# One 64-column decode step for the eight delta-net heads of a hybrid decoder, with the state update placed beside the branch projections

## The chip, the cores and the metric

The kernel is one launch on 1 core of one Trainium2 chip. The metric is device time in microseconds (us), the median of three runs. Nothing of the computation is split over cores, so one span and one chain of waits tell the whole story.

## The reference, cut to what matters

One layer of a hybrid decoder is computed for 256 prompt tokens and 8 sample sequences of one token each. The 264 token columns go through the same weights together: a half-step SwiGLU, a mixer (gated delta-net and sliding-window attention, each projected and merged under a gate), a cross attention over 256 memory tokens, and a second SwiGLU. The change is in the sample tokens' part of the delta-net, which for one token per sequence is a single step per head on a 128 x 128 state:

```python
S_t = a_t (I - b_t k_t k_t^T) S_{t-1} + b_t k_t v_t^T
o_t = S_t^T q_t
o_g = rms_norm(o_t, gdn_norm) * silu(z)
```

There are 8 heads and 8 sample sequences, so 64 such steps, and 64 new states (4 MB in all) must be written out. The query and key are l2-normalised first. In the kernel's form one needs the products of the old state with k and q, then u = b (v - a S^T k), the output from S^T q and the dot product of k and q, and the new state a S + k u^T.

## The kernel before, in words

All activations lie transposed: 128 channels on the partitions, 264 token columns. A weight matrix is streamed once from memory in 512 KB pieces. `wsplit` (L157) loads a piece on SyncE's queue into `raw` (4 buffers), ScalarE rounds it to `wh` (L162, 3 buffers) and VectorE computes the remainder `wl` (L163, 4 buffers). `gemm` (L177) then issues three matmuls for each 128 x 128 block, wh with xh, wh with xl and wl with xh (L194 to L196). These lines are called the weight matmuls below, and everything else on TensorE the small matmuls. Weight matmuls fill TensorE for nearly the whole launch.

The mixer (L285) is where other work must fit in between. It lists its steps in a string, "c0 c1 s c2 w0 c3 w1 x w2 w3":

- `c0` to `c3`: for a pair of heads, `conv_pair` (L452) projects k, q, v and the gate z, applies the short convolution, and leaves them in `kp`, `qp`, `vp`, `zp`. `gdn_pair` (L479) does the chunked delta rule of the 256 prompt tokens, a long chain of small matmuls and VectorE steps that ends with a reciprocal square root (thirteen short VectorE operations), a scaling (L652), four transposes (L655) and the write of `og` (L656). `gdn_sample` (L658) then does the decode step of the pair's 16 columns.
- `s`: the projections for sliding-window attention. `w0` to `w3`: `swa_prompt` (L806) for one group of key heads, in three blocks of scores (L821), softmax, transposes (L842) and values (L848). `x`: `swa_sample` (L852), which goes through the caches in four pieces for the keys (L877) and four for the values (L907), in the three `kc` buffers; the row of the newest value is written into each value piece by a second transfer (L903).

After the steps come sixteen projections of the gate logits (`gate`, L914), of which twelve belong to the stage of the small work and the last four follow once buffers are handed over; then the two branch projections (`branches`, L936) and the output projection `w_out`.

`gdn_sample` as it stands, for each pair of heads: four states of 256 KB are loaded on SyncE's queue (L672) into the pair's own work buffers `d`, `T`, `U`, `bv`; one matmul with a matrix of ones sums squares (L689); four matmuls of 32 columns by 512, one for each loaded state, write four different groups of 32 partitions of one accumulator (L698); a mask and two additions pick the wanted parts; a transpose (L704) brings them back; u is formed, transposed (L719) and written to a small tensor `ud` in device memory (L723); the outputs are normalised (L726 sums the squares) and go to `og`. Then each `ud` row is loaded back, spread over 128 partitions (L737), into `ke` and `u`, ScalarE scales state and spread row (L740, L741, eight operations for each 256 KB), VectorE adds them (L742) and GpSimd's queue stores the new state (L743).

The order of the work is not the order of the code. A list scheduler in the build sets each engine's order from the data dependences, the buffers (a tile of a pool is taken in program order and waits until the tile before it in the same buffer is done with) and its own timing. Each engine then runs its list strictly in order: what waits at the head holds all that stands behind it.

Of the kernel before, what the change touches and what calls it, by code (L numbers as in the profile page):

```python
# [6 lines left out]
F32 = mybir.dt.float32  # L7
# [8 lines left out]
P = 128  # L16
# [53 lines left out]
def bc(ap, n):  # L70
    return ap[:, :, None].to_broadcast([ap.shape[0], ap.shape[1], n])
# [6 lines left out]
class Build:  # L78
# [206 lines left out]
    def mixer(self, norm, nxt):  # L285
# [7 lines left out]
        self.gp = self.mid.enter_context(self.phase("gp", 2))  # L293
        gates = [(n, g) for n in range(2) for g in range(8)]
        if True:
            with self.phase("mc") as mc, self.phase("gd", 2, PSUM) as gd, self.phase("sw", 2, PSUM) as sw:
                self.mc, self.gd, self.sw = mc, gd, sw
                self.c = mc.tile([P, C_N - P], F32, name="c")
                nc.gpsimd.dma_start(out=self.c, in_=i["cst"][:, P:])
                self.scalars_load()  # L300
                self.gemm_ba(win, xs)
                self.conv_state_load()
                for step in "c0 c1 s c2 w0 c3 w1 x w2 w3".split():
                    k = int(step[1:] or 0)
# [18 lines left out]
            with self.phase("bp", 3) as bp:  # L323
# [36 lines left out]
    def gemm_ba(self, win, xs):  # L360
# [65 lines left out]
        nc.vector.tensor_copy(out=self.sbg.rearrange("p a h b -> p (a h b)"), in_=pb[:, 0:128])  # L426

# [230 lines left out]
    def gdn_sample(self, p):  # L658
        nc, mc, o, i = self.nc, self.mc, self.o, self.i
        idn = self.K(C_ID)  # L660
        hsl = slice(2 * p, 2 * p + 2)
        sc = slice(NP, TOK)
        n = 2 * NS
        TT = nc.vector.tensor_tensor
        STT = nc.vector.scalar_tensor_tensor
        st = lambda name, m=n: mc.tile([P, m], F32, name=name)
        v2 = lambda t: t.rearrange("p (h b) -> p h b", h=2)
        Ss = []
        for h in range(2):
            for hb in range(2):  # L670
                S = self.gt(("d", "T", "U", "bv")[h * 2 + hb])
                nc.sync.dma_start(out=S, in_=i["state_gdn"][2 * p + h, :, hb * 4:hb * 4 + 4])  # L672
                Ss.append(S)
        kqz = self.gt("w", 2)[:, 0].rearrange("p (m c) -> p m c", m=4)
        nc.vector.memset(kqz[:, :, 8:32], 0.0)
        kq = kqz[:, :, 0:8].rearrange("p (h r) (b two) -> p h r b two", h=2, two=2)
        cp = lambda src: src.rearrange("p h (r b) -> p h r b", r=2)
        f2 = lambda t: t.rearrange("p (h r b) -> p h r b", h=2, r=2)
        pr = mc.tile([P, 3, n], F32, name="pr")
        vs = st("vs")  # L680
        nc.vector.tensor_copy(out=kq[:, :, :, :, 0], in_=cp(self.kp[:, :, sc]))
        nc.vector.tensor_copy(out=kq[:, :, :, :, 1], in_=cp(self.qp[:, :, sc]))
        nc.vector.tensor_scalar(out=v2(vs), in0=self.vp[:, :, sc], scalar1=0.5, scalar2=None, op0=ALU.mult)
        kk, qq = self.kp[:, :, sc], self.qp[:, :, sc]
        TT(out=v2(pr[:, 0]), in0=kk, in1=kk, op=ALU.mult)
        TT(out=v2(pr[:, 1]), in0=qq, in1=qq, op=ALU.mult)
        TT(out=v2(pr[:, 2]), in0=kk, in1=qq, op=ALU.mult)
# [11 lines left out]
        xm, own = self.gt("E1"), self.gt("sq")[:, 0]
        TT(out=xm, in0=pX.rearrange("p (b e) -> p b e", b=4), in1=bc(self.K(C_DG, 4), P), op=ALU.mult)  # L700
        TT(out=xm[:, 0:2], in0=xm[:, 0:2], in1=xm[:, 2:4], op=ALU.add)
        TT(out=own, in0=xm[:, 0], in1=xm[:, 1], op=ALU.add)
        pk = self.gdt()
        nc.tensor.transpose(pk[:, 0:P], own, idn)  # L704
        pks = pk[:, 0:P].rearrange("p (h r c) -> p h r c", h=2, r=2)[:, :, :, 0:8].rearrange("p h r (b two) -> p h r b two", two=2)
# [16 lines left out]
        ud = self.dr.tile([n, P], F32, name=f"ud{p}")  # L722
        nc.gpsimd.dma_start(out=ud, in_=ut)  # L723
# [7 lines left out]
        TT(out=self.og[:, hsl, sc], in0=v2(of), in1=self.zp[:, :, sc], op=ALU.mult)
        for h in range(2):
            for hb in range(2):
                S = Ss[h * 2 + hb]
                ub = self.gt(("ke", "u")[hb])
                r0 = h * NS + hb * 4
                nc.sync.dma_start(out=ub, in_=ud[r0:r0 + 4, :].rearrange("(o r) e -> o r e", o=1).to_broadcast([P, 4, P]))  # L737
                for b in range(4):
                    bb = hb * 4 + b
                    nc.scalar.mul(out=S[:, b], in_=S[:, b], mul=self.sbg[:, 1, 2 * p + h, bb:bb + 1])  # L740
                    nc.scalar.mul(out=ub[:, b], in_=ub[:, b], mul=kq[:, h, hb, b, 0:1])  # L741
                TT(out=S, in0=S, in1=ub, op=ALU.add)  # L742
                nc.gpsimd.dma_start(out=o["gdn_s"][2 * p + h, :, hb * 4:hb * 4 + 4], in_=S)  # L743
# [192 lines left out]
    def branches(self, bp, sp):  # L936
# [5 lines left out]
        for g in range(8):  # L942
# [19 lines left out]
            self.gemm(i["w_br_swa"], g * 256, 256, sp["os"], ev_s)  # L962
        return ms
# [364 lines left out]
```

## Time and profile before

| | |
|---|---|
| median of 3 runs | 2486.36 us (2486.01 to 2492.16) |
| profiled execution | 2489.28 us |
| its span, first to last instruction | 2487.4 us |
| TensorE busy in the span | 2439.9 us, 98% |
| ScalarE, VectorE busy | 1119.0 us (45%), 1502.1 us (60%) |
| mean granted TensorE clock | 0.989 of full speed |
| mean memory traffic | 183 GB/s |

A view of the profile that groups by time gives busy time of each engine in a stretch; a view that lists instructions in order gives start, duration and, in brackets, the idle time before one and what ended it. [...] A matmul's duration in the list contains the pipeline's depth: the step from one weight matmul to the next is about 0.12 us, while each is listed with 0.28 us.

### The profile page before, as it was taken

The page shows a single profiled execution, that of the slowest core. Times are in us where ns is not written, and L with a number is a line of the kernel's source. Part 1 is how long each engine was busy: PE and PEld are TensorE (multiplying, and loading weights), DVE is VectorE, ACT ScalarE, POOL GpSimd, SP SyncE. Part 2 cuts the span into 40 slices and gives each one's busy share as a digit, 9 for nine tenths or more (in the row PEclk, how much of TensorE's full clock was granted, in tenths as well). Part 3 has the DMA queues.
Part 4 walks back from the last instruction along what each step waited for, and adds up shares of the span by engine and source line. Part 5 has one row for each costly group of instructions (what it writes and reads, how often), then busy time and mean ns, then how long its engine had stood idle before and what let it go on. Part 6 is the DMA issues. An engine that isn't in the chain of part 4 may idle for free.

```text
span 2487.4 us, 47887 instructions
## 1 busy us (share of the span) xinstructions
PE 2439.9 (98%) x19804; PEld 2389.4 (96%) x19804; DVE 1502.1 (60%) x2571; ACT 1119.0 (45%) x1711; POOL 67.3 (3%) x127
## 2 busy tenths in 40 slices
PE   8999999999999999999998999999999999999997
PEld 8999999999999999998997999979999999999997
DVE  6555544555556877876665776668555544555554
ACT  5444333444444545545563555445444333444443
POOL 0000000000000000001010210000000000000000
PEclk9999999999999999998998999999999999999999
DMA  6665566565566457554453876756556666666554
GB/s 212 187 181 179 175 182 186 179 180 181 174 181 206 146 172 234 163 169 155 150 188 126 271 222 205 248 183 184 181 178 180 177 179 185 180 182 181 176 171 130
DMA packets 136091, 455.21 MB, mean 183 GB/s; under 512 B 16736, under 2 KB 22976, under 8 KB 135824
## 3 DMA queue, kind: packets, MB, share of 16 engines
q1 hardware_dynamic: 127936, 426.35, 56.6%
q0 software_dynamic: 7504, 24.65, 2.8%
q8 instruction: 155, 2.54, 0.4%
q10 hardware_dynamic: 432, 1.15, 0.1%
q14 instruction: 64, 0.52, 0.1%
HBM read 438.02 MB, written 14.98 MB: 182 GB/s over the span
## 4 chain that ended last, share of the span: by engine, by line
PE 87%; issue 9%; DMA 2%; DVE 1%; ACT 1%; POOL 0%; SPq 0%; DVEq 0%; POOLq 0%; ACTq 0%
PE mm L194 17%; PE mm L196 17%; PE mm L195 17%; PE mx L196 11%; PE mx L194 11%; PE mx L195 11%; PE mm L1012 0%; DMA ke<-ud 0%; PE mm L1014 0%; PE mm L1013 0%; ACT wh L162 0%; DMA x<-in_x_dram 0%; DMA raw<-in_w_in_dram 0%; PE ap L1068 0%; DVE wl L163 0%
## 5 line engine op out<-in xcount | busy, mean ns | idle before, releaser
L163 DVE TENSOR_TENSOR wl<-raw,wh 128x1024 fp32r<-128x1024 f32 (+2 forms) x794 | 952.0, 1200 | 767.8 <-ACT wh L162 761.9
L162 ACT CAST wh<-raw 128x1024 fp32r<-128x1024 f32 (+2 forms) x794 | 817.2, 1030 | 1187.0 <-PE mm L195 614.8
L194 PE MATMUL mm<-xh,wh 128*128 128x264 f32 x2672 | 769.3, 289 | 11.6 <-ACT wh L162 7.1
L196 PE MATMUL mm<-xh,wl 128*128 128x264 f32 x2672 | 765.1, 288 | 2.7 <-DVE wl L163 2.7
L195 PE MATMUL mm<-xl,wh 128*128 128x264 f32 x2672 | 766.9, 287 | 0.0
L194 PEld LDWEIGHTS mm<-xh,wh 128*128 128x128 f32 x2672 | 508.1, 190 | 17.0 <-ACT wh L162 8.0
L196 PEld LDWEIGHTS mm<-xh,wl 128*128 128x128 f32 x2672 | 506.9, 190 | 8.5 <-DVE wl L163 4.0
L195 PEld LDWEIGHTS mm<-xl,wh 128*128 128x128 f32 x2672 | 508.2, 190 | 3.2 <-issue 2.4
L194 PE MATMUL mx<-xh,wh 128*128 128x264 f32 x1424 | 407.0, 286 | 0.4 <-ACT sut L721 0.4
L196 PE MATMUL mx<-xh,wl 128*128 128x264 f32 x1424 | 406.9, 286 | 0.0
L195 PE MATMUL mx<-xl,wh 128*128 128x264 f32 x1424 | 406.2, 285 | 0.0
L194 PEld LDWEIGHTS mx<-xh,wh 128*128 128x128 f32 x1424 | 270.5, 190 | 0.5 <-ACT sut L721 0.5
L195 PEld LDWEIGHTS mx<-xl,wh 128*128 128x128 f32 x1424 | 270.0, 190 | 0.0
L196 PEld LDWEIGHTS mx<-xh,wl 128*128 128x128 f32 x1424 | 269.8, 189 | 0.0
L196 PE MATMUL mm<-hh,wl 128*128 128x264 f32 x748 | 212.7, 286 | 0.0
L194 PE MATMUL mm<-hh,wh 128*128 128x264 f32 x748 | 212.4, 284 | 0.0
L195 PE MATMUL mm<-hl,wh 128*128 128x264 f32 x748 | 212.3, 284 | 0.0
L196 PE MATMUL mx<-hh,wl 128*128 128x264 f32 x660 | 187.6, 285 | 0.0
L194 PE MATMUL mx<-hh,wh 128*128 128x264 f32 x660 | 187.5, 284 | 0.0
L195 PE MATMUL mx<-hl,wh 128*128 128x264 f32 x660 | 187.4, 284 | 0.0
L195 PEld LDWEIGHTS mm<-hl,wh 128*128 128x128 f32 x748 | 140.9, 188 | 0.0
L194 PEld LDWEIGHTS mm<-hh,wh 128*128 128x128 f32 x748 | 140.6, 188 | 0.0
(562 smaller groups left out, 2834.5 us busy)
## 6 DMA issues: line engine op xcount, KB each, us to landing
raw<-in_ffn_w_dram SPq DMA_DIRECT2D x511, 512.0 KB, 3.7
raw<-in_w_in_dram SPq DMA_DIRECT2D x152, 512.0 KB, 3.8
raw<-in_w_out_dram SPq DMA_DIRECT2D x32, 512.0 KB, 4.0
raw<-in_ffn_w_dram SPq DMA_DIRECT2D x33, 256.0 KB, 2.6
raw<-in_w_br_gdn_dram SPq DMA_DIRECT2D x16, 512.0 KB, 4.7
raw<-in_w_br_swa_dram SPq DMA_DIRECT2D x16, 512.0 KB, 4.8
gd<-gt POOLq DMA_DIRECT2D x32, 132.0 KB, 3.0
tg<-gd POOLq DMA_DIRECT2D x32, 132.0 KB, 4.6
```

The lines of the kernel that those rows point to most:

```text
L162: self.last_h = nc.scalar.copy(out=H, in_=raw)
L163: self.last_l = nc.vector.tensor_tensor(out=L, in0=raw, in1=H.bitcast(F32), op=ALU.subtract)
L194: nc.tensor.matmul(acc, wh, xh, start=(kg + c == 0), stop=False)
L195: nc.tensor.matmul(acc, wh, xl, start=False, stop=False)
L196: nc.tensor.matmul(acc, wl, xh, start=False, stop=(kg + c == nk - 1))
```

## The change

`gdn_sample` is no longer called for each pair. `sample_cols` copies each pair's 16 sample columns of k, q, v and z into collecting tiles of 64 columns, and one `gdn_sample` for all eight heads runs after the last pair's projections and ahead of that pair's `gdn_pair`. Its vector steps work on 64 columns. The states are loaded on GpSimd's queue into the three `kc` buffers, one for each 32 x 512 matmul, and are not kept. The state update is taken out into `state_update`, called 16 times: once for each block of the branch projections and once for each block of `w_out`. Each call loads 256 KB of old state a second time (`Su`, two buffers), loads the spread `ud` rows (`ub`, one buffer), both on GpSimd's queue, and does the eight ScalarE scalings, the addition and the store as before.

```diff
+        self.kS, self.gS = (self.gp.tile([P, 8, NS], F32, name=nm, bufs=1) for nm in ("kS", "gS"))
...
+                self.qS, self.vS, self.zS = (mc.tile([P, 8, NS], F32, name=nm) for nm in ("qS", "vS", "zS"))
...
                     if step[0] == "c":
                         self.conv_pair(win, xs, k)
+                        self.sample_cols(k)
+                        if k == 3:
+                            self.gdn_sample()
                         self.gdn_pair(k)
-                        self.gdn_sample(k)
...
                     self.gemm(i["w_out"], g * 256, 256, ms, lambda j, ps, g=g: ev_x(g * 2 + j, ps))
+                    self.state_update(bp, 8 + g)
...
-    def gdn_sample(self, p):
+    def sample_cols(self, p):
+        nc = self.nc
+        for src, dst in ((self.kp, self.kS), (self.qp, self.qS), (self.vp, self.vS), (self.zp, self.zS)):
+            nc.vector.tensor_copy(out=dst[:, 2 * p:2 * p + 2], in_=src[:, :, NP:TOK])
...
-        n = 2 * NS
+        n = 8 * NS
...
-                S = self.gt(("d", "T", "U", "bv")[h * 2 + hb])
-                nc.sync.dma_start(out=S, in_=i["state_gdn"][2 * p + h, :, hb * 4:hb * 4 + 4])
...
-        for m in range(4):
-            nc.tensor.matmul(pX[32 * m:32 * m + 32, :], kqz[:, m], Ss[m].rearrange("p b e -> p (b e)"), start=True, stop=True)
...
+        for p in range(4):
+            kqz = mc.tile([P, 4, 32], F32, name="kqz")
...
+            for m in range(4):
+                Sm = self.kc_tile()
+                nc.gpsimd.dma_start(out=Sm, in_=i["state_gdn"][2 * p + m // 2, :, (m % 2) * 4:(m % 2) * 4 + 4].rearrange("d (x b) e -> d x (b e)", x=2))
+                nc.tensor.matmul(pX[32 * m:32 * m + 32, :], kqz[:, m], Sm.rearrange("p a b -> p (a b)"), start=True, stop=True)
+            xm = mc.tile([P, 4, P], F32, name="sc")
...
+    def state_update(self, bp, q):
+        nc, i, o = self.nc, self.i, self.o
+        h, hb = q // 2, q % 2
+        S, ub = (bp.tile([P, 4, P], F32, name=nm, bufs=k) for nm, k in (("Su", 2), ("ub", 1)))
+        r0 = h * NS + hb * 4
+        nc.gpsimd.dma_start(out=S, in_=i["state_gdn"][h, :, hb * 4:hb * 4 + 4])
+        nc.gpsimd.dma_start(out=ub, in_=self.ud[r0:r0 + 4, :].rearrange("(o r) e -> o r e", o=1).to_broadcast([P, 4, P]))
+        for b in range(4):
+            c = hb * 4 + b
+            nc.scalar.mul(out=S[:, b], in_=S[:, b], mul=self.gS[:, h, c:c + 1])
+            nc.scalar.mul(out=ub[:, b], in_=ub[:, b], mul=self.kS[:, h, c:c + 1])
+        nc.vector.tensor_tensor(out=S, in0=S, in1=ub, op=ALU.add)
+        nc.gpsimd.dma_start(out=o["gdn_s"][h, :, hb * 4:hb * 4 + 4], in_=S)
...
             self.gemm(i["w_br_swa"], g * 256, 256, sp["os"], ev_s)
+            self.state_update(bp, g)
```

Line numbers below L300 move: a line of the prompt part such as L608 stands six lines further on, and one of the attention part such as L877 nine.

**The order on TensorE, end of the small work.** Before: the last rows of pair 3 and of its decode step, from the last weight matmul (L196) on; `gd` is the small work's accumulator, and L689 to L726 are the decode step.

```order
L196 MATMUL mm<-xh,wl 128x264
L608 MATMUL gd<-Pm,T 64x64 x4
L613 MATMUL gd<-bv,U 128x128 x2
...
L637 MATMUL gd<-u,ke 128x128 x2
L655 MATMUL gd<-idn,d 128x128 x4
L689 MATMUL gd<-pr,ones 128x48
L698 MATMUL gd<-d,w 32x512
...
L719 MATMUL gd<-idn,su_13922 16x128
L726 MATMUL gd<-stt,ones 128x16
```

In the change, the same place from the last weight matmul before it (`sw` is the attention's accumulator; L886 and L916 are the keys and values of `swa_sample`, L830, L851 and L857 belong to `swa_prompt`, the rest to pair 3):

```order
L196 MATMUL mm<-xh,wl 128x264
L583 MATMUL gd<-Pm,d 32x64 x4
L857 MATMUL sw<-pT,Vt 64x128 x4
L886 MATMUL sw<-qb,kc 128x8 x8
...
L905 MATMUL sw<-idn,kcT 128x128
L600 MATMUL gd<-Pm,T 128x64 x4
L916 MATMUL sw<-kcT,kc 128x8 x11
...
L916 MATMUL sw<-kcT,kc 128x8 x4
L614 MATMUL gd<-Pm,T 64x64 x4
...
L661 MATMUL gd<-idn,d 128x128 x4
```

Between two weight matmuls stood 34 small ones, 18 of which wait for a semaphore; now 125 stand there, 43 of which wait, and `swa_sample`, a block of `swa_prompt` and two more doubling levels of pair 3 have moved into that place. Further down a second such place appears, 24 matmuls of `swa_prompt` for the last group, 11 of which wait, just ahead of the branches; before, the branches began while weight matmuls of the gates still ran.

**The order on TensorE, state products.** Before, four rows L698 stand together, four times in all. In the change each L703 stands alone:

```order
L703 MATMUL gd<-kc,kqz 32x512
L195 MATMUL mm<-xl,wh 128x264
L196 MATMUL mm<-xh,wl 128x264
L194 MATMUL mm<-xh,wh 128x264
L195 MATMUL mm<-xl,wh 128x264
L196 MATMUL mm<-xh,wl 128x264
L194 MATMUL mm<-xh,wh 128x264
L195 MATMUL mm<-xl,wh 128x264
L703 MATMUL gd<-kc,kqz 32x512
```

Seven weight matmuls lie between these two, the closest of the sixteen; from one use of a `kc` buffer to the next it is 55 to 101.

**The order on GpSimd's queue, branches.** Before, this queue held the loads `tg` of the gates one behind the other. In the change, one block of the branches:

```order
L752 DMA out_gdn_s_dram<-Su 128x512
L746 DMA ub<-ud 128x512
L956 DMA tg<-gd_6_15641 128x264
L956 DMA tg<-gd_7_15647 128x264
L745 DMA Su<-in_state_gdn_dram 128x512
L956 DMA tg<-gd_8_14703 128x264
```

A store, which waits for VectorE's addition, and a load, which waits for ScalarE to be done with `ub`, now stand ahead of gate loads.

## Rows read from the trace of the kernel before

**Rows 1.** The page: busy time of all engines; the chain that ended last.

```profile
PE 2439.9 (98%) x19804; PEld 2389.4 (96%) x19804; DVE 1502.1 (60%) x2571; ACT 1119.0 (45%) x1711; POOL 67.3 (3%) x127
PE 87%; issue 9%; DMA 2%; DVE 1%; ACT 1%; POOL 0%; SPq 0%; DVEq 0%; POOLq 0%; ACTq 0%
```

**Rows 2.** Stretches: length, PE, PEld, DVE, ACT, POOL busy, granted clock, DMA share, GB/s.

```profile
980.00:1000.00 20.00, 18.90 (x154) 18.20 (x154) 16.87 (x48) 14.70 (x35) 2.14 (x4) 1.00 0.84 290
1120.00:1140.00 20.00, 13.92 (x95) 12.06 (x93) 15.85 (x74) 15.21 (x48) 3.57 (x7) 0.83 0.31 108
1170.00:1180.00 10.00, 10.00 (x74) 9.24 (x72) 4.14 (x7) 1.41 (x3) 0.52 (x1) 0.71 0.28 95
1330.00:1360.00 30.00, 17.91 (x119) 14.08 (x119) 14.76 (x67) 9.07 (x26) 1.60 (x4) 0.75 0.25 82
1370.00:1390.00 20.00, 18.78 (x152) 18.37 (x151) 15.74 (x27) 15.57 (x35) 6.42 (x12) 1.00 0.86 296
1420.00:1470.00 50.00, 50.00 (x413) 50.00 (x412) 34.91 (x53) 22.27 (x28) 9.56 (x18) 1.00 0.74 225
```

**Rows 3.** TensorE in order of time, pair 3's end and decode step.

```profile
1303.56 0.32 PE L577 MATMUL gd<-Pm,d 128*32 128x64 f32 x8
...
1335.22 0.28 PE L196 MATMUL mm<-xh,wl 128*128 128x264 f32 x1
1335.44 0.68 PE L608 MATMUL gd<-Pm,T 64*64 64x64 f32 x8
...
1347.26 1.11 PE L655 MATMUL gd<-idn,d 128*128 128x128 f32 x4 [5.08 <-DVE d L652]
...
1358.04 0.59 PE L194 MATMUL mx<-xh,wh 128*128 128x264 f32 x1 [0.36 <-ACT sut L721]
1358.42 0.42 PE L195 MATMUL mx<-xl,wh 128*128 128x264 f32 x1
```

**Rows 4.** The same view, the stretch behind the decode step of pair 1.

```profile
1115.97 0.70 PE L821 MATMUL sw<-kd,qr 64*128 64x256 f32 x2
...
1122.24 0.29 PE L196 MATMUL mm<-xh,wl 128*128 128x264 f32 x1
...
1126.86 0.67 PE L848 MATMUL sw<-pT,Vt 128*64 128x128 f32 x8
...
1133.04 0.59 PE L194 MATMUL mm<-xh,wh 128*128 128x264 f32 x1 [4.44 <-DVE cy L921]
```

**Rows 5.** The same view, the four state products of a pair between weight matmuls.

```profile
1116.82 0.28 PE L195 MATMUL mm<-xl,wh 128*128 128x264 f32 x1
1117.04 0.62 PE L698 MATMUL gd<-d,w 128*32 128x512 f32 x1
...
1117.06 0.62 PE L698 MATMUL gd<-bv,w 128*32 128x512 f32 x1
1117.49 0.59 PE L698 MATMUL gd<-d,w 128*32 128x512 f32 x1
...
1118.03 0.39 PE L196 MATMUL mm<-xh,wl 128*128 128x264 f32 x1
```

**Rows 6.** The chain of waits, its piece of the cache keys: start, duration.

```profile
1147.43 2.77 PE sw L877 x24
```

**Rows 7.** Transfers: count, size, median us from issue to landing.

```profile
tg<-gd POOLq DMA_DIRECT2D x32, 132.0 KB, 4.6
og<-in_mem_dram POOLq DMA_DIRECT2D x4, 512.0 KB, 5.4
d<-in_state_gdn_dram SPq DMA_DIRECT2D x4, 256.0 KB, 3.6
kc<-in_cache_v_dram SPq DMA_DIRECT2D x4, 256.0 KB, 4.5
kc<-vn POOLq DMA_DIRECT2D x4, 2.0 KB, 2.5
```

**Rows 8.** Groups by line, 800 to 1500 us: count, busy us, mean ns, idle before.

```profile
L162 ACT CAST wh<-raw 128x1024 fp32r<-128x1024 f32 x186 | 194.2, 1048 | 209.7 <-PE mm L195 169.3 <-issue 25.4 <-DVE sry L150 3.6
L741 ACT ACTIVATE ke<-ke,w 128x128 f32<-128x128 f32 x32 | 10.2, 390 | 14.4 <-DMA ke<-ud 14.4
L947 POOL DMA_DIRECT2D tg<-gd x32 | 17.2, 537 | 63.1 <-DVE m L952 31.4 <-DVE m L956 27.9 <-DMA out_gdn_s_dram<-bv 3.8
```

More of the change, by code (lines that the diff above doesn't have):

```diff
@@ L426, in gemm_ba @@
         nc.vector.tensor_copy(out=self.sbg.rearrange("p a h b -> p (a h b)"), in_=pb[:, 0:128])
+        nc.vector.tensor_copy(out=self.gS, in_=self.sbg[:, 1])
     def conv_group(self, win, xs, t0, dst):
@@ L660, in gdn_sample @@
+    def gdn_sample(self):
+        nc, mc, i = self.nc, self.mc, self.i
         idn = self.K(C_ID)
[L661 to L663 removed]
+        n = 8 * NS
         TT = nc.vector.tensor_tensor
         STT = nc.vector.scalar_tensor_tensor
[L666 to L670, printed above, removed]
[L671 to L673 removed]
@@ L674, in gdn_sample @@
[L674 to L687, printed above, removed]
+        fl = lambda t: t.rearrange("p h b -> p (h b)")
+        kk, qq, vv, zz = (fl(t) for t in (self.kS, self.qS, self.vS, self.zS))
+        ch = self.kc_tile().rearrange("p a (b c) -> p (a b) c", b=2)
@@ L688, in gdn_sample @@
+        ss, rr, cy, ct = (ch[:, k] for k in range(4))
+        buf = mc.tile([P, 2, P], F32, name="kcT", bufs=2).rearrange("p a (b c) -> p (a b) c", b=2)
+        pr, of = buf[:, 0:3], buf[:, 3]
+        TT(out=pr[:, 0], in0=kk, in1=kk, op=ALU.mult)
+        TT(out=pr[:, 1], in0=qq, in1=qq, op=ALU.mult)
+        TT(out=pr[:, 2], in0=kk, in1=qq, op=ALU.mult)
         ps = self.gdt()
         nc.tensor.matmul(ps[:, 0:3 * n], self.ones, pr.rearrange("p a b -> p (a b)"), start=True, stop=True)
-        ss, rr, dq = st("sss", 2 * n), st("srr", 2 * n), st("sdq")
+        buf = mc.tile([P, 2, P], F32, name="kcT", bufs=2).rearrange("p a (b c) -> p (a b) c", b=2)
@@ L699, in gdn_sample @@
[L699 to L705, printed above, removed]
@@ L706, in gdn_sample @@
-        be = self.sbg[:, 0, hsl, :].rearrange("p h b -> p (h b)")
-        ga = self.sbg[:, 1, hsl, :].rearrange("p h b -> p (h b)")
-        u, u2, t, of = st("su"), st("su2"), st("stt"), st("sof")
+        for p in range(4):
+            kqz = mc.tile([P, 4, 32], F32, name="kqz")
+            nc.gpsimd.memset(kqz[:, :, 8:32], 0.0)
+            kq = kqz[:, :, 0:8].rearrange("p (h r) (b two) -> p h r b two", h=2, two=2)
+            for two, src in enumerate((self.kS, self.qS)):
+                nc.vector.tensor_copy(out=kq[:, :, :, :, two], in_=src[:, 2 * p:2 * p + 2].rearrange("p h (r b) -> p h r b", r=2))
+            pX = self.gdt()
+            for m in range(4):
[3 more added lines that the diff above has]
+            xm = mc.tile([P, 4, P], F32, name="sc")
+            TT(out=xm, in0=pX.rearrange("p (b e) -> p b e", b=4), in1=bc(self.K(C_DG, 4), P), op=ALU.mult)
+            TT(out=xm[:, 0:2], in0=xm[:, 0:2], in1=xm[:, 2:4], op=ALU.add)
+            TT(out=xm[:, 0], in0=xm[:, 0], in1=xm[:, 1], op=ALU.add)
+            pk = self.gdt()
+            nc.tensor.transpose(pk[:, 0:P], xm[:, 0], idn)
+            pks = pk[:, 0:P].rearrange("p (h r c) -> p h r c", h=2, r=2)[:, :, :, 0:8].rearrange("p h r (b two) -> p h r b two", two=2)
+            for two in range(2):
+                dst = sx[:, two, p * 16:p * 16 + 16].rearrange("p (h r b) -> p h r b", h=2, r=2)
+                nc.vector.tensor_copy(out=dst, in_=pks[:, :, :, :, two])
@@ L726, in gdn_sample @@
         nc.tensor.matmul(pn[:, 0:n], self.ones, t, start=True, stop=True)
-        so, rn = st("sso"), st("srn")
+        so, rn = ss[:, 0:n], ss[:, n:2 * n]
         nc.vector.tensor_scalar(out=so, in0=pn[:, 0:n], scalar1=1.0 / P, scalar2=EPS, op0=ALU.mult, op1=ALU.add)
-        self.rsqrt(mc, rn, so, "sn")
+        self.rsqrt(mc, rn, so, "sn", y=cy[:, 0:n], t=ct[:, 0:n])
         STT(out=of, in0=of, scalar=self.gn, in1=rn, op0=ALU.mult, op1=ALU.mult)
[L731 to L743, printed above, removed]
+        TT(out=self.og[:, :, NP:TOK], in0=of.rearrange("p (h b) -> p h b", h=8), in1=self.zS, op=ALU.mult)
+    def state_update(self, bp, q):
[11 more added lines that the diff above has]
+        nc.gpsimd.dma_start(out=o["gdn_s"][h, :, hb * 4:hb * 4 + 4], in_=S)
     def swa_proj(self, win, xs):
```

23 lines of the change are left out of this document (12 added, 11 removed).

## The prediction

> **What bounds the kernel now.** I read the page first. TensorE is busy 98% of the span and holds 87% of the chain that ends last, and "issue", its own pauses, holds 9% [rows 1]. VectorE and ScalarE have slack on average, so an operation taken from them is worth nothing by itself. What counts is whether TensorE gets its next weight matmul: a small matmul between weight matmuls costs its own time on TensorE, and its wait costs only what no weight matmul fills.
>
> The second view is the stretches, to see where filling fails [rows 2]. From 1420 to 1470 us all is filled: 413 matmuls in 50 us, 0.121 us each, my price of a weight matmul. [...]
>
> The third view is TensorE's list in order of time. Between the weight matmuls at 1335.22 and 1358.04 there are 22.8 us without one [rows 3]. The first part, 1335.44 to the end of L655 at 1348.4, is pair 3's own tail, 12.9 us; the decode step of pair 3 is the other 9.7 us. The first weight matmul behind is released by ScalarE's copy of u (L721), the second is listed with 0.42 us against 0.28: the clock is still low. The second gap is 1122.24 to 1133.04, 10.8 us [rows 4], where `swa_prompt`'s chain stands alone. Both are places where the stock of weight matmuls was used up while a chain had still to run.
>
> **The change, part by part.** The weight matmuls stay as many as they were, so the question is how much small work is left when the twelve gates are used up. By the order on TensorE it is more: 125 small matmuls in one place (call it A), 43 with a wait, against 34 with 18, and 24 with 11 waits in a second place ahead of the branches (call it B). The 64-column step comes ahead of pair 3's chain and of `swa_sample`, with which it shares the `kc` buffers, and takes gate matmuls with it. These terms decide.
>
> *Removed.* The gap of 22.8 us, pair 3's tail included, which I book again under A [rows 3]. The idle time of 6.1 us at 1120 (20.0 less 13.92) and 1.1 plus 1.2 us at 980 and 1370 [rows 2]: I let all of it go, though some may return elsewhere. About 4 us of low clock: 2.9 at 1170 (0.29 of 10 us) and some 1 at 1120. Small work that stood between weight matmuls and now lies in A and B: of the 125, some 22 are pair 3's tail and are counted already; of the others 64 are the narrow cache matmuls, at 2.77 / 24 = 0.115 us [rows 6], 7.4 us; some 39 in A and 24 in B at 0.16, a value between 0.68 / 8 = 0.085 for L608 and 1.11 / 4 = 0.28 for L655 [rows 3], 10 us. Together 17. Sum removed: 22.8 + 6.1 + 2.3 + 4 + 17 = 52.
>
> *A.* Its lower end is pair 3's chain with nothing to wait for but itself: the tail of 12.9 us, plus the earlier levels. These ran from L577 at 1303.56 to 1335.22, 31.7 us with 217 weight matmuls in the order between, worth 26.3, so 5.4 were not weight matmuls [rows 3]; with the 7.4 of cache matmuls, 26 us. The upper end is the pace of a wait in bare stretches: 22.8 / 18 = 1.27 us or 10.8 / 11 = 0.98, times 43, 42 to 55 us. It is nearer to neither: two chains, pair 3 and `swa_sample`, alternate there and cover each other, but `swa_sample` has loads of its own in a row. Eight pieces go through three buffers, so at least two rounds wait for one that has just been freed, 4.5 us each, and a value piece gets its new row by a second transfer of 2.5 us [rows 7]. I take 38.
>
> *B.* 11 waits at 0.98 are 10.8 us, as in rows 4. Its two blocks of scores, softmax and values took 11.5 us each from L821 at 1115.97 to L848's end at 1127.5 [rows 4], partly beside weight matmuls; 23 if not overlapped. I take 14.
>
> *State products.* Before, four L698 write the four column groups of the array side by side: the gap from the weight matmul at 1116.82 to the one at 1118.03 is 1.21 us, 1.09 without that matmul's own step, and the four starts (two at 1117.05, the others about 0.45 later) overlap in it [rows 5]. Now each of sixteen stands alone between weight matmuls. No row shows one alone. The lower bound is a quarter of the gap, 0.27 (no extra cost); the upper bound is the whole gap, if the four were truly parallel: 16 x 1.09 - 4 x 1.09 = +13.1. I take the upper one, since the rows show overlap and not a sequence. [...]
>
> *Restarts.* After each of two bare stretches the clock is low for some 4 us, as after the one at 1358, where I count half of it as lost: two where one was, +2 [rows 3].
>
> *Branches.* ScalarE gets eight scalings of 0.39 us per block, 3.1 us [rows 8]. A block of 96 weight matmuls lasts 11.6 us, in which ScalarE is 45% busy (22.27 of 50) and VectorE 70% [rows 2]; so about 72% for ScalarE. There is room for it; if the cover went, each scaling ahead of a cast (1.05 us, L162 [rows 8]) would delay the weights. The three transfers per block wait on GpSimd's queue: a store for VectorE's addition, a load for ScalarE to free `ub`; behind them stand gate loads of 4.6 us [rows 7]. I put in +1, ends 0 and 4. The shorter vector work, four steps made into one, I cost at nothing: VectorE has slack, and where it does not it lies in the gaps booked above.
>
> Sum added: 38 + 14 + 13 + 2 + 1 = 68. Net 68 - 52 = +16. The profiled execution took 2489.3 us, 2.9 more than the median of the runs; 2486.4 + 16 = 2502.
>
> **Rivals.** *R1, faster:* pair 3's chain covers `swa_sample`, so A is only its lower end 26, B 11, and a state product alone costs 0.27: 26 + 11 + 0 + 2 + 1 = 40, less 52, -12: 2474. The bare gap of rows 3 speaks for it, since 9.7 us of it are the decode step alone and go. Against it is the order, which puts more waits where no weight matmul is. It decides at A below about 30 with cheap products.
>
> *R2, no change:* A 30, B 11 and products half way, +7: 30 + 11 + 7 + 2 + 1 = 51 against 52; 2485.
>
> *R3, worse:* the queue of GpSimd. The sixteen state loads need 0.54 us of issue [rows 8] and 4.6 to 5.4 us to land [rows 7], against 55 weight matmuls, 6.7 us, from one use of a buffer to the next at the closest: 0.8 us to spare. If they come late, some thirteen by a further 1 to 2 us, TensorE stands at each: +13 to +26, 2515 and more. In the branches the one `ub` buffer has the same form, 5.9 us of load plus 3.1 of scalings in 11.6. For it speaks that these loads share the queue with gate loads, against it that L947's issues took 0.54 us in the mean with VectorE mostly busy. [...]
>
> *R4, the step does not take effect as meant:* if the wait for A's loads runs past 50 us, the result is that of R3 without its cause.
>
> **How the numbers follow.** About 0.3%, 7.5 us, is what a measurement of this kernel can tell from no change. My forecast, 2494 to 2514, has 0.45; R1 0.15; R2 0.22; R3 0.13 and R4 0.05. Slower is 0.45 + 0.13 + 0.05 = 0.63, same 0.22, faster 0.15. The unknown terms are A (26 to 55), B (11 to 23) and the products (0 to 13). The range leaves out most of R1's lower half and the far ends of R3 and R4: 2477 to 2521. Of the slower cases alone it would be 2494 to 2521.
>
> **What would show it.** Right: in the changed kernel's TensorE list a stretch without weight matmuls of 32 to 45 us behind the twelfth gate, ending with L661, with waits on `kc` loads and on VectorE in turn; a second one of 11 to 18 us with L830 to L857 ahead of the branches; about 1.1 us from weight matmul to weight matmul round each L703; nothing bare at 1120 or in a decode step; granted clock low only behind A and B; blocks of the branches at 11.6 us with TensorE full. Wrong: A at 26 or less or L703 at 0.3 (R1); idle time ahead of L703 ended by a `kc` load on GpSimd's queue, or ScalarE's scalings waiting for `ub` with casts late behind them (R3).

## The result, and the profile after

The changed kernel takes 2513.85 us (median of 4 runs, 2511.39 to 2514.83) against 2486.49: 1.1% slower, ratio 1.011 with an interval of 1.0098 to 1.0122. The forecast was slower, 2502; the time lies inside the range, but 27 us were lost where 16 were expected. Three of the terms that add time were too small, one of them (A) with the wrong mechanism, and what was removed was more than booked; the errors partly cancelled.

The page of the changed kernel, busy time and the chain that ended last (answers to [rows 1]):

```profile
PE 2461.7 (98%) x19789; PEld 2398.0 (95%) x19789; DVE 1489.4 (59%) x2459; ACT 1117.9 (45%) x1708; POOL 92.0 (4%) x176
...
PE 90%; DMA 3%; issue 2%; DVE 2%; ACT 1%; POOL 1%; SPq 0%; DVEq 0%; POOLq 0%; ACTq 0%
PE mm L194 17%; PE mm L196 17%; PE mm L195 17%; PE mx L194 10%; PE mx L196 10%; PE mx L195 10%; DMA out_gdn_s_dram<-Su 1%; PE gd L703 1%; DVE wl L163 1%; PE sw L830 1%; DMA ub<-ud 1%; PE mm L1022 0%; DMA cth<-cy 0%; PE mm L1024 0%; PE mm L1
```

TensorE is busy 21.8 us longer with fewer instructions, "issue" fell from 9% to 2%, and among the names new in the chain are the store of `Su`, the load of `ub`, and the state product L703. A page like this says "more TensorE time, same work", which is no wait. The lone state products below are 12.7 us of it; the rest is a first hint at the clock.

Both programs have 18,240 weight matmuls of L194 to L196. In some 500 places, from the 6,411th to the 10,958th, another one stands at the same number, so there the n-th tells how many are done and not which. I compare the start of the n-th, after less before: -0.9 us for the 6,400th (799 us in before), -4.5 for the 8,400th, -36.5 for the 9,600th (1315 us), +13.5 for the 10,000th, +13.6 for the 10,400th (1443 us), +20.9 for the 10,800th, +24.4 for the 11,200th and from there to the end. (The trace of before is of an execution 2.9 us longer than its median, so all these differences may be too small by about that.) The changed kernel is 36 us *ahead* in the use of its weight matmuls when the gates are nearly used up, falls back 50 us within the next 400, and loses 11 more in the branches.

The places of the fall, on TensorE's list: start, duration, idle time before and what ended it. First the stretch A (answers to [rows 3]), 1302.55 to 1348.50; here and below a stretch is counted from the start of the last L194 ahead of it, 0.24 us more than from the last L196:

```profile
1302.55 0.28 PE L194 MATMUL mm<-xh,wh 128*128 128x264 f32 x1
...
1303.85 1.95 PE L886 MATMUL sw<-qb,kc 128*128 128x8 f32 x16
...
1305.86 1.72 PE L886 MATMUL sw<-qb,kc 128*128 128x8 f32 x8
...
1314.32 1.94 PE L595 MATMUL gd<-U,E 128*128 128x64 f32 x8 [1.35 <-DVE U L589]
...
1318.54 4.81 PE L916 MATMUL sw<-kcT,kc 128*128 128x8 f32 x22
...
1345.30 1.06 PE L661 MATMUL gd<-idn,d 128*128 128x128 f32 x4
...
1348.50 0.59 PE L194 MATMUL mx<-xh,wh 128*128 128x264 f32 x1
```

The idle times of the whole list of A add up to about 8 us, and no `kc` load ends one. Then B, where the last attention group stands alone and waits twice for ScalarE's softmax, 1385.16 to 1404.28:

```profile
1392.16 1.12 PE L851 MATMUL sw<-idn,sc 128*128 128x128 f32 x4 [4.18 <-ACT sc L846]
...
1400.68 1.11 PE L851 MATMUL sw<-idn,sc 128*128 128x128 f32 x4 [4.01 <-ACT sc L846]
1402.47 1.13 PE L857 MATMUL sw<-pT,Vt 128*64 128x128 f32 x8 [0.68 <-ACT pT L852]
1404.28 0.81 PE L194 MATMUL mm<-ogh,wh 128*128 128x264 f32 x2 [0.68 <-ACT ogh L203]
```

The view of stretches (columns as in [rows 2]) tells what kind of loss A is, and shows B and the branches:

```profile
1302.80:1305.70 2.90, 2.90 (x36) 2.49 (x35) 0.84 (x3) 0.27 (x1) 0.00 (x0) 1.00 0.18 72
1306.00:1333.00 27.00, 24.25 (x139) 21.67 (x138) 8.76 (x31) 2.90 (x11) 2.06 (x4) 0.50 0.18 50
1333.10:1343.00 9.90, 5.86 (x42) 4.35 (x41) 4.44 (x22) 5.87 (x22) 0.56 (x1) 1.00 0.03 13
...
1348.50:1353.50 5.00, 5.00 (x20) 4.29 (x19) 1.52 (x2) 1.05 (x1) 0.00 (x0) 0.50 0.01 2
...
1385.00:1404.00 19.00, 8.67 (x46) 5.09 (x44) 6.17 (x18) 8.15 (x23) 5.84 (x11) 0.66 0.48 154
1404.30:1408.50 4.20, 4.20 (x20) 4.20 (x21) 4.20 (x13) 4.20 (x14) 0.00 (x0) 0.54 0.00 0
```

```profile
1470.00:1560.00 90.00, 84.46 (x662) 82.43 (x662) 65.83 (x115) 65.42 (x141) 20.11 (x38) 0.98 0.84 275
```

In A's middle TensorE is busy 24.25 of 27 us. It hardly waits; it works at a granted clock of 0.50 of full speed. (The profile models the ends of matmuls, so the share is not exact; the few idle times in the list say the same.) Behind A and behind B the first weight matmuls still run at the low clock, 20 in 5.00 us (at 0.50) and 20 in 4.20 (at 0.54). B is what a bare chain was thought to be: 8.7 busy of 19. In the branches the clock is nearly full, 0.98, and TensorE still idles 5.5 of 90 us.

The state products, each alone between weight matmuls (answers to [rows 5]; the list shows one product as two instructions, x2):

```profile
1196.36 0.28 PE L195 MATMUL mm<-xl,wh 128*128 128x264 f32 x1
1196.57 1.04 PE L703 MATMUL gd<-kc,kqz 128*32 128x512 f32 x2
1197.55 0.39 PE L196 MATMUL mm<-xh,wl 128*128 128x264 f32 x1
```

From L195 to L196 pass 1.19 us, 1.07 more than a weight matmul's own 0.12. Sixteen of them are 17.1 us; before, four groups of four were 4.4.

### The profile page after: what moved, and what is told of

It is laid out like the page before. It is cut to its first block, busy times and chain, and to the rows that moved or that the text cites. A ratio compares the mean times of both kernels' runs of the same rounds, so it can differ in the third digit from the quotient of the medians.

```text
span 2511.8 us, 47758 instructions
## 1 busy us (share of the span) xinstructions
PE 2461.7 (98%) x19789; PEld 2398.0 (95%) x19789; DVE 1489.4 (59%) x2459; ACT 1117.9 (45%) x1708; POOL 92.0 (4%) x176
## 4 chain that ended last, share of the span: by engine, by line
PE 90%; DMA 3%; issue 2%; DVE 2%; ACT 1%; POOL 1%; SPq 0%; DVEq 0%; POOLq 0%; ACTq 0%
PE mm L194 17%; PE mm L196 17%; PE mm L195 17%; PE mx L194 10%; PE mx L196 10%; PE mx L195 10%; DMA out_gdn_s_dram<-Su 1%; PE gd L703 1%; DVE wl L163 1%; PE sw L830 1%; DMA ub<-ud 1%; PE mm L1022 0%; DMA cth<-cy 0%; PE mm L1024 0%; PE mm L1023 0%
## 5 line engine op out<-in xcount | busy, mean ns | idle before, releaser
L163 DVE TENSOR_TENSOR wl<-raw,wh 128x1024 fp32r<-128x1024 f32 (+2 forms) x794 | 952.1, 1200 | 773.4 <-ACT wh L162 768.4
L162 ACT CAST wh<-raw 128x1024 fp32r<-128x1024 f32 (+2 forms) x794 | 817.3, 1030 | 1185.0 <-PE mm L195 599.4
L194 PE MATMUL mm<-xh,wh 128*128 128x264 f32 x2672 | 766.6, 287 | 6.4 <-ACT wh L162 6.4
L195 PE MATMUL mm<-xl,wh 128*128 128x264 f32 x2672 | 763.9, 286 | 0.0
L196 PE MATMUL mm<-xh,wl 128*128 128x264 f32 x2672 | 763.2, 287 | 0.5 <-DVE wl L163 0.4
L194 PEld LDWEIGHTS mm<-xh,wh 128*128 128x128 f32 x2672 | 505.6, 189 | 13.5 <-ACT wh L162 7.3
L196 PEld LDWEIGHTS mm<-xh,wl 128*128 128x128 f32 x2672 | 503.9, 189 | 10.7 <-issue 8.9
L195 PEld LDWEIGHTS mm<-xl,wh 128*128 128x128 f32 x2672 | 505.2, 189 | 4.1 <-issue 2.8
L196 PE MATMUL mx<-xh,wl 128*128 128x264 f32 x1424 | 407.4, 286 | 0.0
L194 PE MATMUL mx<-xh,wh 128*128 128x264 f32 x1424 | 407.4, 286 | 0.0
L195 PE MATMUL mx<-xl,wh 128*128 128x264 f32 x1424 | 406.4, 285 | 0.0
L194 PEld LDWEIGHTS mx<-xh,wh 128*128 128x128 f32 x1424 | 270.7, 190 | 0.8 <-issue 0.6
L196 PEld LDWEIGHTS mx<-xh,wl 128*128 128x128 f32 x1424 | 269.9, 190 | 0.6 <-issue 0.6
L195 PEld LDWEIGHTS mx<-xl,wh 128*128 128x128 f32 x1424 | 270.2, 190 | 0.0
L196 PE MATMUL mm<-hh,wl 128*128 128x264 f32 x748 | 212.7, 286 | 0.0
L194 PE MATMUL mm<-hh,wh 128*128 128x264 f32 x748 | 212.4, 284 | 0.0
L195 PE MATMUL mm<-hl,wh 128*128 128x264 f32 x748 | 212.3, 284 | 0.0
L196 PE MATMUL mx<-hh,wl 128*128 128x264 f32 x660 | 187.6, 285 | 0.0
L194 PE MATMUL mx<-hh,wh 128*128 128x264 f32 x660 | 187.5, 284 | 0.0
L195 PE MATMUL mx<-hl,wh 128*128 128x264 f32 x660 | 187.3, 284 | 0.0
L195 PEld LDWEIGHTS mm<-hl,wh 128*128 128x128 f32 x748 | 140.9, 188 | 0.0
L194 PEld LDWEIGHTS mm<-hh,wh 128*128 128x128 f32 x748 | 140.6, 188 | 0.0
```

Of the source, the lines that this page charges most:

```text
L162: self.last_h = nc.scalar.copy(out=H, in_=raw)
L163: self.last_l = nc.vector.tensor_tensor(out=L, in0=raw, in1=H.bitcast(F32), op=ALU.subtract)
L194: nc.tensor.matmul(acc, wh, xh, start=(kg + c == 0), stop=False)
L195: nc.tensor.matmul(acc, wh, xl, start=False, stop=False)
L196: nc.tensor.matmul(acc, wl, xh, start=False, stop=(kg + c == nk - 1))
```

## The experiments

I held a theory against a rival. **Shared tiles:** a tile is taken in program order, so the decode step, which stands ahead of pair 3's chain and of `swa_sample` and uses their `kc`, `sc` and `gd` tiles, makes them late; they are left over when the gates are used up. **Added work:** the lone products and the update beside the branches are simply more to do, wherever the step stands. For the branches: **casts held**, a scaling on ScalarE that waits for its load holds the weight casts behind it. All ratios are to the kernel before on the same chip (2485 us); the 2513.85 us of the changed kernel were taken beside 2486.49, so differences from it are good to 1 or 2 us.

**Where the step stands.** First, `swa_sample` ahead of the last pair:

```diff
-for step in "c0 c1 s c2 w0 c3 w1 x w2 w3".split():
+for step in "c0 c1 s c2 w0 x c3 w1 w2 w3".split():
```

> The order of the steps is changed so that swa_sample (x) and its kc loads come before the projections of pair 3 and before the decode step. Theory 'shared tiles': the decode step holds kc, sc and the two gd banks in program order, so what is written behind it (swa_sample, the attention groups, pair 3's chain) starts late and is left over when the gates run out. Then with x ahead the second stretch (19.1 us) goes, the first (46 us) keeps pair 3's chain and shrinks to 35 to 42 us: 2490 to 2502 us. Rival 'added work': the sixteen lone state products (1.05 us each in the trace of the changed kernel) and the update beside the branches make the loss, wherever the step stands: 2508 us or more.

Measured: 2497.33 us, ratio 1.0043 (1.0027 to 1.0060). B shrank from 19.1 to 2.3 us and A from 46.0 to 30.0, a larger cut than named; the time still lies in the range since small work now costs its time between weight matmuls: at the 9,600th this version is 21 us ahead of before, where the changed kernel was 36. What is left in A is pair 3's chain. It shows the clock's part too:

```profile
1318.97 1.10 PE L595 MATMUL gd<-U,E 128*128 128x64 f32 x8 [0.64 <-DVE U L589]
1320.83 1.97 PE L600 MATMUL gd<-Pm,T 128*128 128x64 f32 x8 [0.75 <-DVE Pm L597]
```

The same eight matmuls L595 take 1.10 us here and 1.94 in the changed kernel, at a granted clock of 0.50 (1314.3 to 1316.3 us); in before, as L589 at 1323.03, they took 1.00 at a clock of 1.00. L600 just behind it, of the same shape, takes 1.97 here, as it does in the changed kernel at 0.50.

Second, the decode step last of all:

```diff
-for step in "c0 c1 s c2 w0 c3 w1 x w2 w3".split():
+for step in "c0 c1 s c2 w0 c3 w1 x w2 w3 d".split():
...
-        if k == 3:
-            self.gdn_sample()
...
+    elif step[0] == "d":
+        self.gdn_sample()
```

> The decode step is put last in the program order of the mixer, behind pair 3 and all attention groups; the rest is as in the changed kernel. Shared tiles: both stretches (46.0 and 19.1 us) go, about 22 us of small matmuls in them return between weight matmuls; a new stretch of some 25 us appears for the last eight state products, whose loads go round three kc buffers at some 5.5 us each: 2494 to 2504 us. Added work: 2508 us or more.

Measured: 2500.26 us, 1.0056 (1.0039 to 1.0073). Both stretches are gone, and the new one is there as expected, 23.4 us. Its rows show what it waits for:

```profile
1326.51 1.05 PE L703 MATMUL gd<-kc,kqz 128*32 128x512 f32 x4
1330.75 2.85 PE L703 MATMUL gd<-kc,kqz 128*32 128x512 f32 x4 [3.19 <-DMA kc<-in_state_gdn_dram]
1335.29 0.45 PE L709 MATMUL gd<-idn,sc 128*128 128x128 f32 x1 [1.69 <-DVE sc L707]
...
1340.89 3.07 PE L703 MATMUL gd<-kc,kqz 128*32 128x512 f32 x4 [1.77 <-DMA kc<-in_state_gdn_dram]
```

So the step's loads through few buffers have only moved to the end. In the branches this version loses 18 us (from -6.8 at the 10,000th weight matmul to +11.1 at the 11,200th), 7 more than the changed kernel; its ScalarE waits there too, 22.6 us for `ub` and 18.3 for `Su`. Third, the same with eight other buffers:

```diff
-Sm = self.kc_tile()
+Sm = self.gt((("d", "T", "U", "bv"), ("ke", "u", "E1", "sq"))[p % 2][m])
...
+Ss.append(Sm)
...
+for m, Sm in enumerate(Ss):
     nc.tensor.matmul(pX[32 * m:32 * m + 32, :], kqz[:, m], Sm.rearrange("p a b -> p (a b)"), start=True, stop=True)
```

> As the run with the decode step last, and the sixteen states are loaded into eight of the pair's work tiles (d, T, U, bv and ke, u, E1, sq), so that four loads go out at once and the four products of a pair of heads stand together. Shared tiles: no stretch without weight matmuls is left, and the products cost about 1.1 us for four instead of 1.05 each (13 us less): 2458 to 2472 us. Added work: only the 13 us of the products come off, 2498 to 2503 us.

Measured: 2466.36 us, 0.9921 (0.9906 to 0.9935): now faster than before, as the shared tiles had it. No stretch is left in the mixer's end, and the four products run side by side:

```profile
1294.93 0.28 PE L196 MATMUL mm<-xh,wl 128*128 128x264 f32 x1
1295.14 0.62 PE L706 MATMUL gd<-d,kqz 128*32 128x512 f32 x1
1295.15 0.62 PE L706 MATMUL gd<-T,kqz 128*32 128x512 f32 x1
1295.15 0.62 PE L706 MATMUL gd<-U,kqz 128*32 128x512 f32 x1
1295.16 0.62 PE L706 MATMUL gd<-bv,kqz 128*32 128x512 f32 x1
...
1296.13 0.39 PE L194 MATMUL mm<-xh,wh 128*128 128x264 f32 x1
```

From weight matmul to weight matmul 1.20 us, 1.08 for four; alone in the changed kernel 1.07 for one. A lone product costs as much as four.

Which of the shared things is it, the buffers of the states or the place? The same eight tiles, with the step left where the change put it:

> The decode step stays where the change puts it, ahead of pair 3's chain, but its states go into the eight work tiles of the pair instead of the three kc buffers. This asks which shared tile it is. If kc (its sixteen loads one behind the other, and swa_sample behind them) holds everything up, the first stretch falls to some 15 us with 23 small matmuls by the order, the second goes, and four products stand together (13 us less): 2466 to 2482 us. If the place in the program is what counts (the two gd banks, sc), pair 3's chain is still left over: 2490 us or more.

Measured: 2480.81 us, 0.9982 (0.9973 to 0.9991), inside the first of the two ranges. Of the 33 us gained on the changed kernel 12.8 are the grouped products (17.1 less 4.3), and A falls from 46.0 to 10.4 us, B from 19.1 to 11.7. Together these are 56, as much of A's small work only moves between weight matmuls: 36 rows of it are left in A, where 230 were. So leaving the `kc` buffers, with the grouping that eight tiles allow, is worth more than the place; the place is worth the other 14 us, 2480.8 against 2466.4 (with `kc` it was 13.6, 2513.9 against 2500.3). Which of the `gd` banks and the `sc` tile holds pair 3 was not taken apart.

**The branches.** The update is left out, so that the new states are not written:

```diff
-self.state_update(bp, g)
-self.state_update(bp, 8 + g)
```

> The sixteen calls of the state update are left out (the new states are not written); the rest is as in the changed kernel. Theory 'casts held': the 11 us that the weight matmuls lose between 1410 and 1560 us come from ScalarE, which stands at a scaling that waits for its ub or Su load while weight casts stand behind it: 2502 to 2504 us, branches without a gap. Rival 'nothing there': the loss in the branches is the clock after the second stretch or the memory traffic of the weights themselves: 2510 us or more.

Measured: 2499.14 us, 1.0056 (1.0041 to 1.0071): 14.7 us less than the changed kernel, some 3.5 more than named. In the branches next to nothing is lost now: the count of weight matmuls stands at +8.6 us at the 10,000th and at +8.8 from the 10,400th to the end, and TensorE is full from 1404 to 1550 us. What goes beyond 11 us arose ahead of them: some 2 us before the 9,600th weight matmul, and 2.6 from there to the 10,000th, where the granted clock behind A is full at once (1.00 from 1345.97 to 1353) and was 0.50 for 5 us in the changed kernel. Why is open. The branches:

```profile
1404.00:1550.00 146.00, 146.00 (x1202) 146.00 (x1200) 105.91 (x175) 73.40 (x103) 17.11 (x32) 1.00 0.70 222
```

What ends the waits there is told by ScalarE's waits from 1408 to 1570 us in the changed kernel (total us, times, longest), and by its list and GpSimd's:

```profile
ACT ub L750 <- DMA ub<-ud: 23.1, 11, 6.7
ACT Su L749 <- DMA Su<-in_state_gdn_dram: 12.4, 7, 3.1
```

```profile
1473.62 2.10 ACT L162 CAST wh<-raw 128x1024 fp32r<-128x1024 f32 x2
1482.41 1.28 ACT L750 ACTIVATE ub<-ub,kS 128x128 f32<-128x128 f32 x4 [6.68 <-DMA ub<-ud]
1483.59 1.03 ACT L162 CAST wh<-raw 128x1024 fp32r<-128x1024 f32 x1
```

```profile
1471.70 0.69 DVE L751 TENSOR_TENSOR Su<-Su,ub 128x512 f32<-128x512 f32 x1
...
1483.72 0.69 DVE L751 TENSOR_TENSOR Su<-Su,ub 128x512 f32<-128x512 f32 x1 [6.33 <-ACT ub L750]
```

```profile
1475.45 0.54 POOL L752 DMA_DIRECT2D out_gdn_s_dram<-Su  x1 [5.13 <-DVE m L961]
1475.99 0.54 POOL L746 DMA_DIRECT2D ub<-ud  x1
...
1481.12 0.54 POOL L745 DMA_DIRECT2D Su<-in_state_gdn_dram  x1 [3.54 <-DMA out_gdn_s_dram<-Su]
```

```profile
1484.67 0.39 PE L194 MATMUL mx<-osh,wh 128*128 128x264 f32 x1 [1.16 <-ACT wh L162]
```

The buffer `ub` is free at 1472.39, when the addition before has ended, but its load goes out only at 1475.99, behind a store that stood at the head of GpSimd's list, and lands 6.4 us later. ScalarE has been through its casts since 1475.7 and stands idle for 6.68 us until 1482.41 with a weight cast next in its list; TensorE idles for that cast. VectorE stands as long at the addition behind the scaling, with a remainder L163 to come, and over the branches TensorE's waits name that remainder (4.7 us in all) more than the cast (1.6). The load of `Su` waits for the store before it to land. This is one mechanism in these rows. The order is the remedy: the scalings come behind the last weight cast of their block, so that the load has had the time of a block (`last_h` is the last L162 issued, `after` in the call).

```diff
-self.state_update(bp, g)
+self.state_update(bp, g, self.last_h)
...
+with self.tc.issue_after(after.ins):
     nc.scalar.mul(out=S[:, b], in_=S[:, b], mul=self.gS[:, h, c:c + 1])
     nc.scalar.mul(out=ub[:, b], in_=ub[:, b], mul=self.kS[:, h, c:c + 1])
```

> The changed kernel with one more order: ScalarE's eight scalings of a block come behind the last weight cast of that block, so that their loads have had the time of a block. Casts held: the 11 us of the branches fall to 0 to 3 us: 2502 to 2507 us. If it is the number of scalings or of transfers and not the wait at the head of ScalarE's list: 2511 us or more.

Measured: 2502.10 us, 1.0068 (1.0051 to 1.0084), 11.8 less than the changed kernel with the same 128 scalings and 48 transfers. By the count of weight matmuls 2.8 us are lost in the branches (10,000th to 11,200th) where 10.9 were; the other 2.4 us between the two traces stood ahead of them. ScalarE's waits for `ub` in the same stretch, with none for `Su` left:

```profile
ACT ub L751 <- DMA ub<-ud: 2.4, 1, 2.4
```

Together with the step last and in eight tiles:

> The decode step last in the program, states in eight work tiles (2466.4 us, with 8.8 us lost in the branches), and the scalings spaced as above. Casts held: 2457 to 2461 us. Otherwise 2465 us or more.

Measured: 2453.18 us, 0.9872 (0.9857 to 0.9886), 4 us better than named; the fastest version. Counted from the 10,000th weight matmul the version without spacing had lost 12.0 us in the branches, not 8.8, and this one loses 1.2; another 2.5 us of the difference stood ahead of the mixer in these two traces. Two stretches of it:

```profile
1280.00:1320.00 40.00, 40.00 (x326) 35.71 (x325) 29.35 (x77) 15.86 (x23) 8.48 (x18) 1.00 0.69 228
1320.00:1400.00 80.00, 78.79 (x643) 78.23 (x642) 57.06 (x100) 48.00 (x90) 23.01 (x43) 1.00 0.82 272
```

No bare stretch, and a clock of 1.00 in both, where before had 22.8 us without a weight matmul.

**The other half of the change alone.** The decode step stays pair by pair, as before; only the update goes to the branches:

```diff
     self.gemm(i["w_br_swa"], g * 256, 256, sp["os"], ev_s)
+    self.state_update(bp, g)
...
 def gdn_sample(self, p):
...
-    nc.sync.dma_start(out=ub, in_=ud[r0:r0 + 4, :].rearrange("(o r) e -> o r e", o=1).to_broadcast([P, 4, P]))
...
-    TT(out=S, in0=S, in1=ub, op=ALU.add)
-    nc.gpsimd.dma_start(out=o["gdn_s"][2 * p + h, :, hb * 4:hb * 4 + 4], in_=S)
```

> The other half of the change alone: the decode step runs pair by pair as before, with four products together, but the update is taken out of it and stands beside the branches with its second load, as in the changed kernel. If the update in the mixer held the work tiles d, T, U, bv until its stores had landed, as the chain of before shows once (a store of bv, 4.0 us, ahead of pair 3's bv), then the stretch of 22.8 us and the 6 idle us at 1120 go and the branches cost 9 to 11 us: 2462 to 2476 us. If the stretch of before was pair 3's own chain, it stays: 2490 us or more.

Measured: 2486.36 us, 1.0006 (0.9997 to 1.0015): between the two, so neither expectation holds. The trace says why in part; its execution, 2482.84 us, was the fastest of ten, so it looks 6 us better against the trace of before than the medians do. It is 15.6 us ahead of before at the 10,000th weight matmul (of which 2.7 arose ahead of the mixer) and gives 9.2 back by the 11,200th, in the branches. Behind the last gate stands a stretch of 14.9 us, from 1326.49 to 1341.43, not 22.8. It is the end of pair 3 and its decode step:

```profile
1330.80 1.11 PE L659 MATMUL gd<-idn,d 128*128 128x128 f32 x4 [3.78 <-DVE d L656]
...
1334.64 1.03 PE L703 MATMUL gd<-d,w 128*32 128x512 f32 x1 [2.44 <-DVE sry L155]
...
1341.43 0.59 PE L194 MATMUL mx<-xh,wh 128*128 128x264 f32 x1 [0.27 <-DVE sso L734]
```

I had left the decode step's own latency out of the expectation. With the scalings spaced:

> The decode step pair by pair with the update beside the branches (2486.4 us, 9.2 us lost in the branches by the trace), and the scalings spaced behind the last weight cast of their block. Casts held: the loss in the branches falls to 1 or 2 us: 2477 to 2480 us, clearly faster than before; what then still divides it from the 64-column step placed last (2453.2 us) is the bare stretch of 14.9 us behind pair 3 and the waits of four decode steps in place of one. If the branches were not what ate the gain: 2484 us or more.

Measured: 2477.40 us, 0.9972 (0.9961 to 0.9982), as expected. So the update beside the branches is worth 8 us once it holds up no cast, and the 64-column step, placed last and with its eight tiles, another 24 (2477.4 to 2453.2). With the scalings spaced but the step where the change puts it, it costs 25 (2477.4 to 2502.1).

Last, the best version with `swa_sample` ahead of `w0`, `c3` and `w1`, three places earlier in the string:

> The best version so far (step last, eight work tiles, spaced) with swa_sample one step earlier, ahead of the first attention group. Shared tiles: nothing is left bare in that version, so an earlier swa_sample frees nothing that TensorE waits for: 2450 to 2456 us. If chains still compete for kc and the sw banks: 2447 us or less, or 2460 or more.

Measured: 2459.14 us, 0.9893 (0.9878 to 0.9908), between the ranges. Of the 6.4 us by which its trace falls behind the best version's, 3.4 arise before the 5,600th weight matmul, ahead of everything that was edited, and 2.6 in the mixer. It frees nothing, but whether it costs anything by itself is open. The same holds for offsets of up to 4 us ahead of the mixer in all these programs: their cause was not sought, and differences of that size between two traces are not read as the work of an edit.

## Why the prediction was right or wrong

**The bound** was right: what TensorE lost and regained set the time, its gaps and, as A shows, its clock. That nothing taken from VectorE pays by itself was not tested alone.

**A** (38 us, 26 to 55): 46.0, so the size was within the bounds but the mechanism was not. I priced it as 43 waits at the pace of the bare stretches. The rows show few waits: 24.25 of 27 us busy in its middle, at 0.50. Of the 46 us about 8 are idle, and half of the 24.25 us at the low clock, some 12, is what the clock cost by my estimate, from the 0.50 alone. The step that failed is the use of durations from rows at a granted clock of 1.00 (L608 at 1335.44 and L877 at 1147.43 in before) for matmuls that the change pushes into one place, with waits on `kc` loads put where the clock belonged. I took 0.115 us for a narrow cache matmul [rows 6]; there, eight L886 take 1.72 us at 0.50, 0.215 each. By x_early's rows L595 is 1.10 against 1.94. And the covering of pair 3 and `swa_sample` by each other did happen, as the few waits show.

**B** (14, 11 to 23): 19.1, two waits of 4 us for the softmax, at a mean clock of 0.66. It was mis-sized by 5 us.

**State products** (+13.1): 17.1 less 4.4 is 12.7. Right, and for the reason given, the overlap in the rows: between two weight matmuls four products side by side cost 1.08 us (the version with eight tiles) and one alone 1.07 (the changed kernel).

**Restarts** (+2): behind A 20 weight matmuls take 5.00 us and behind B 20 take 4.20, where 20 at 0.121 would take 2.4: 2.6 and 1.8 us. Less the one restart booked for before, 2, that is +2.4. Right.

**Branches** (+1, 0 to 4): 10.9 us by the count of weight matmuls, of which the run with the scalings spaced got 8.1 back. This is the worst miss. I judged ScalarE by its share, 72%, and put R3's form, a load that is late for the one `ub`, at a low chance; but what counts is the order in its list. In the row shown the load left late behind a store and landed after 6.4 us, where I had reckoned with 5.9, while ScalarE was already there; so the scaling at the head waited up to 6.7 us with a cast behind it.

**Removed** (52): A, B, products, branches and restarts come to 46.0 + 19.1 + 12.7 + 10.9 + 2 = 90.7; the trace is 24.4 longer in its span, so 66 must have been removed, 14 more than I had; this is a remainder and not a measurement. Part of it is an error of count. Of the 125 matmuls in A, 32 belong to the caches (the list shows each twice, so 64 rows), 26 to pair 3's tail, and 67 are others, where I had 64, 22 and 39; and the 0.68 us of L608 are four matmuls in eight rows, 0.17 each. At 0.17 to 0.28 those 67 and the 24 of B come to 15 to 25 us, where I booked 10: an estimate, and it covers 5 to 15 of the 14. The two misses, 22 us in what is added (90.7 against 68) and 14 in what is removed, partly cancelled. That the time came out inside the range is in part luck.

**The rivals.** R1 did not come: it needed cheap products and A at 26. R3's first form, late state loads ahead of L703, did not come either: TensorE was busy for all of 1180 to 1250 us at a granted clock of 1.00, with every L703 in it. Its second form came, with waits of up to 6.7 us for `ub`: the load at 1475.99 was issued in 0.54 us, as the gate loads of before were [rows 8], but it stood behind a store, and what the load of `Su` waited for is the store ahead of it (3.54 us in the row shown).

## What to carry to other kernels

When a change merges steps, look at what the merged step holds in program order (buffers, banks) and who is queued behind it: here the batch was worth 24 us placed last with eight other tiles, and cost 25 where it stood with three. Price small matmuls that a change pushes together at the durations which rows show at the lower clock: here 0.215 us for a cache matmul at 0.50, against 0.122 at 0.99. A second load with its arithmetic beside a full pipeline is cheap only if the instruction that waits for it stands late enough in its engine's list: here the branches lost 10.9 us, and 2.8 with the scalings behind the last cast of their block. The busy share of ScalarE, which I had put at 72%, did not tell.

## What the runs showed of the hardware that was not expected

The clock inside A. From 1302.80 to 1305.70 us TensorE was busy throughout at 1.00, with the small matmuls L583, L857 and the cache matmuls L886. Then the granted clock fell to 0.50, and it stayed there from 1306 to 1333 us while TensorE was busy for 24.25 of these 27 us. It was 1.00 again from 1333.1 to 1343 us, behind L619 to L629. One line shows the price: sixteen rows of L886 take 1.95 us ahead of the fall, at 0.99, and eight take 1.72 behind it, at 0.50.

In the best version the same cache matmuls (L890 there) stand in shorter bunches between weight matmuls. They run at 1.00, twenty rows in 2.40 us, but behind the bunch the clock falls to 0.50 there too, and the weight matmuls pay, the one shown with 0.42 us against 0.28 (the view of stretches, then two rows of TensorE's list):

```profile
1150.79:1156.00 5.21, 5.21 (x52) 4.83 (x51) 0.94 (x2) 1.01 (x3) 0.00 (x0) 1.00 0.54 167
1156.20:1159.60 3.40, 3.40 (x18) 3.40 (x17) 1.32 (x2) 1.05 (x1) 0.69 (x2) 0.50 0.34 115
```

```profile
1152.20 2.40 PE L890 MATMUL sw<-qb,kc 128*128 128x8 f32 x20
...
1156.48 0.42 PE L196 MATMUL mm<-xh,wl 128*128 128x264 f32 x1
```

TensorE did not idle in either stretch, and [rows 2] had shown the same of the kernel before: busy 10.00 of 10 us from 1170 to 1180 at 0.71. So the price of pushing small matmuls together was here more the level of the clock, some 12 us in A by the estimate above, than the waits, about 8.

And four state products side by side take 1.08 us where one takes 1.07. The rows of before had shown an overlap; that it is complete was the upper bound of the estimate.
